# Attention gates of four heads in one product with tokens in the rows, and all heads' probabilities turned by VectorE, in a fused decoder layer on one Trainium2 core

## The chip, the core and the metric

The kernel runs on one core of one Trainium2 chip. The core has a matrix engine (TensorE, PE in the profile; its weight loads are PEld), and VectorE (DVE), ScalarE (ACT), GpSimd (POOL) and SyncE (SP), which here only issues transfers. The program lists the instructions of each engine in an order of its own; the engines meet at semaphores. Operands lie in on-chip memory with 128 partitions; products land in PSUM, in banks of 128 x 512 float32. POOL's and SP's transfers run on 16 DMA engines.

The metric is the time of one execution on the device in microseconds. Before the change the runs gave a median of 1040.27 us (1040.1 to 1040.35, three runs).

## What is computed

One decoder layer for 256 tokens of width 2048, in float32. What matters here is the attention and its gate; the convolution branch, the merge and the output projection stay as they are.

```python
h = rmsnorm(x, pre_norm_g)
proj = h @ w_in     # q_a 512, c_kv 512, k_rope 64, z_mla 2048, four of 2048 for the convolution, g_mla, g_conv
q = rmsnorm(q_a, q_a_norm_g) @ w_q_b        # 16 heads of 128 + 64
kv = rmsnorm(c_kv, kv_a_norm_g) @ w_kv_b    # 16 heads of 128 (keys) + 128 (values)
p = softmax(causal((q_nope @ k_nope.T + rope(q_rope) @ rope(k_rope).T) / sqrt(192)))
attn = (p @ v) * silu(z_mla)                # per head 256 x 128
y_mla = attn @ w_o_mla
y_conv = (b_gate * conv3(c_gate * c_in) * silu(z_conv)) @ w_o_conv
merged = sigmoid(g_mla) * y_mla + sigmoid(g_conv) * y_conv
return x + rmsnorm(merged @ w_out, post_norm_g)
```

## The kernel before

**Numbers in two halves.** A float32 operand goes into TensorE as a high part, rounded by a copy on ScalarE (`whi`, `hi`), and a low part, the difference, made by VectorE (`wlo`, `lo`). `split_act` (L232) issues the two; VectorE's needs ScalarE's. A `product` (L217) is three matmuls: high by high, high by low, low by high. `halves` (L224) does the same with both halves of the moving operand side by side in 512 columns: one matmul 512 wide and one 256 wide. The first kind of result is complete in a bank; the second lies in two halves of a bank, which `whole` (L378) adds up: a copy of one half by ScalarE (`half`) and an addition by VectorE.

**Weights.** Everything that is multiplied from `w_in`, `w_q_b` and the rest comes in units of 128 x 2048 (1 MB). `plan` (L106) lists them in the order of use. `take(i)` (L203) calls `ahead` (L192): SP has loaded units up to three on (`raw`, three buffers), and units up to one on are split, as two halves of 128 x 1024, into `whi` and `wlo`, five buffers of each (L186, L187). A split of a half can start when its buffer's last reader, a matmul, is done.

**Which order holds.** All of TensorE's instructions are kept in the order of the program (L88), POOL's transfers of the loop too, and the operations that are marked with `keep_in_program_order`. The rest of ScalarE's and VectorE's instructions is put in order by the scheduler of the framework, from its own estimate of times; the order is fixed when the program is built. Buffers are chosen from pools with a fixed number of them, and an operation waits until the one it gets is free.

**The loop.** After the latent projections (`qa`, `ckv`, `kr`) comes the loop over 16 heads (L739). The convolution's four projections have 2048 columns each, and 16 blocks of 512 columns of these are spread over the loop: `channels(h, i)` (L666), i = 0 to 3, is a quarter of the block that belongs to head h, 24 matmuls for each i and two banks `cv` (one for each 128 tokens). After the fourth quarter `channels_done` (L681) takes the banks away: block n = 0 of four by a ScalarE copy, n = 1 and 3 by a VectorE product, n = 2 by a ScalarE sigmoid and a VectorE product. For head h the program has

1. `project` (L387): the product for z of this head, features in the rows and both halves of the tokens in the columns, 16 matmuls 512 wide and 16 of 256, and `silu` (L654): `whole`, `rows` (the norm's factor), a sigmoid on ScalarE, a product.
2. `scores(h)` (L582) and the softmax behind it, on ScalarE and VectorE. From head 2 on the probabilities p are turned (tokens from rows to columns) by `turned` (L304): VectorE transposes blocks of 32 x 32 into `via`, `go` sends it to DRAM by four transfers of POOL (`far`), and `come` brings it back by one into p; `by_rows` and `quarters` are views that put the blocks in place. For heads 0 and 1 three transposes on TensorE do it (`tp`, L631).
3. `channels(h, 0)`, then `values(h - 1)` (L640) of the head before: four matmuls over pt and vv, then `whole` into `at_f` and a product with the gate `sz`.
4. `channels(h, 1)`, `come` for p, `channels(h, 2)`.
5. `made[h]`: the operands of coming heads (`group_a` queries and keys of two heads, `group_r` their rotary part, `group_v` the values of four heads).
6. `channels(h, 3)`, and `turn(h, p)` (L627), which splits the turned p into the halves `pt` (ScalarE, then VectorE; both kept in the program's order).

For the last head of each four (h % 4 == 3) `turn` comes ahead of step 5, and `values(h)` follows in step 5 right behind `group_a`; for head 15 values come at the end of the loop. In between stand the convolution's steps, `taps` (L702) and `channels_join` (L693), which turns a finished block by the same `turned`.

After the loop come the merge (`sq`, L857) and the output projection (`out`, L898). `split_branch` (L814) splits `at_f` there, two heads in one pass.

Of the kernel before, what the change touches and what calls it, by code (L numbers as in the profile page):

```python
# [18 lines left out]
P = 128  # L19
S = 256  # L20
# [62 lines left out]
def tile_layer(ctx: ExitStack, tc: tile.TileContext, xw, x, pos, pvec, post_g, wc, wz, wcv, wkr, wqk, wqr, wv, cwr, wsq, out):  # L83
# [6 lines left out]
    def transpose(*a):  # L90
        return tc.keep_in_program_order(nc.tensor.transpose(*a))  # L91
# [16 lines left out]
    def add(ap, width=UNIT):  # L108
        plan.append((ap, width))
        return len(plan) - 1  # L110
# [5 lines left out]
    u_head, u_grp = [[0] * 5 for _ in range(H)], {}  # L116


    made = {h: [] for h in range(H)}
# [6 lines left out]
    first = [("a", 0), ("r", 0), ("v", 0)]  # L126
    order = []
    for h in range(H):
        order += [(h, 0), (h, 1)] + (first if h == 0 else []) + [(h, 2), (h, 3)] + made[h] + [(h, 4)]
    for i, j in order:  # L130
        if i in ("a", "r", "v"):
            u_grp[i, j] = add({"a": wqk, "r": wqr, "v": wv}[i][j], R if i == "r" else UNIT)
        else:

            u_head[i][j] = add(wcv[i, j - 1] if j else wz[i])

    u_d = [[[add(wsq[n, c, k]) for k in range(4)] for n in range(4)] for c in range(4)]

# [64 lines left out]
    def take(i):  # L203
        ahead(i)
        parts = splits.pop(i)

        def piece(j, n):
            o = j * n
            h, o = o // HALF, o % HALF
            return parts[h][0][:, o : o + n], parts[h][1][:, o : o + n]  # L210

        return piece

    def bank(name, tag="mm", bufs=4):
        return psum.tile([P, 512], F32, name=name, tag=tag, bufs=bufs)
# [88 lines left out]
    def turned(src, via, n):  # L304

        via = via[:, : P * n]
        v = via.rearrange("p (q k x) -> p q k x", q=4, k=n)
        nc.vector.transpose(v.rearrange("p q k x -> p k q x"), src)  # L308
        far = dram.tile([P, P * n], F32, name="far", tag=f"far{n}", bufs=2)

        def go():
            f = far[:, :].rearrange("(q y) (i m) -> i y q m", q=4, i=4)
            for i in range(4):
                m = via[32 * i : 32 * i + 32, :].rearrange("y (q m) -> y q m", q=4)
                tc.keep_in_program_order(nc.gpsimd.dma_start(out=f[i], in_=m))  # L315

        def come(dst):

            tc.keep_in_program_order(nc.gpsimd.dma_start(out=dst, in_=far[:, :]))

        return go, come
# [260 lines left out]
    def scores(h):  # L582
# [35 lines left out]
        for t in range(NT):  # L618
            o = slice(t * P, (2 * t + 1) * P)
            nc.vector.tensor_scalar(p[:, o], p[:, o], rs[:, t : t + 1], None, op0=ALU.mult)  # L620
        if h < 2:
            return p, None
        go, come = turned(p[:, :], temp("via", (P, 3 * P), bufs=1), 3)
        go()
        return p, come

    def turn(h, p):  # L627

        pt = temp("pt", (P, 2, 3 * P), F32R, 1)
        if h < 2:  # L630
# [9 lines left out]
    def values(h, pt, sz):  # L640
# [12 lines left out]

    def silu(name, ps):  # L654
        f, s = temp("sl_f", bufs=1), temp(name)
        whole(f[:, :], ps)
        rows(f[:, :])
        nc.scalar.activation(s[:, :], f[:, :], AF.Sigmoid)
        nc.vector.tensor_tensor(s[:, :], f[:, :], s[:, :], op=ALU.mult)
        return s  # L660


    cv_t = cv_f[:, :, :].rearrange("p (j t k) s -> p j t (k s)", j=4, t=NT)
    cv_ps = {}

    def channels(h, i, between=None):  # L666

        if i == 0:
            cv_ps["now"] = [bank(f"cv{h}_{t}", tag="cv", bufs=2) for t in range(NT)]
        w = take(u_head[h][1 + i])  # L670
        for t in range(NT):
            if t and between:
                between()
            for k4 in range(4):
                k = 4 * i + k4
                a = [x_both[:, k, o + t * P : o + (t + 1) * P] for o in (0, S)]
                product(cv_ps["now"][t][:, :], a, w(k4, 512), k == 0, k == KD - 1)
        if i == 3:
            channels_done(*divmod(h, 4))

# [55 lines left out]

    cv_w = bp.tile([P, NT, 512], F32, name="cv_w")
    tap, coming = None, []
    for h in range(H):  # L739

        tapped = h % 4 == 2 or (h > 0 and h % 4 == 0) or h == H - 1
        sz_new = silu("sz", project(u_head[h][0], f"z{h}"))
        if h == 0:
            latent_turn("qa", qa, "q_g", (("st", 1), ("o", 1)))

            def turn_keys():
                latent_turn("ckv", ckv, "kv_g", (("mm", 4), ("mm", 4)))
                next(table_parts)

            channels(h, 0, turn_keys)  # L750
            for i in first:
                make(*i)
            key_rope()
            channels(h, 1)
            channels(h, 2)
            p, _ = scores(h)
        elif h == 1:

            pt = turn(0, p)
            channels(h, 0)  # L760
            values(0, pt, sz)
            p, _ = scores(h)
            channels(h, 1)
            channels(h, 2)
            pt = turn(h, p)
        else:
            p, come = scores(h)
            while coming:
                coming.pop()()
            channels(h, 0)  # L770
            if h > 2 and h % 4:

                values(h - 1, pt, sz)
            channels(h, 1)
            if tapped:
                next(tap)
            come(p[:, :])
            channels(h, 2)
            if tapped:
                next(tap)  # L780
            if h % 4 == 3:
                pt = turn(h, p)
        for i in made[h]:
            make(*i)
            if i[0] == "a" and (h == 1 or h % 4 == 3):
                values(h, pt, sz_new)
        sz = sz_new
        channels(h, 3)
        if h > 1 and h % 4 != 3:
            pt = turn(h, p)  # L790
        if h == H - 1:
            values(h, pt, sz)
        if h % 4 == 0 and h > 0:
            coming.append(channels_join(h // 4 - 1, 0))
        if h % 4 == 3:
            coming.append(channels_join(h // 4, 1))
        if h % 4 == 1:
            tap = taps(h // 4, 1)
            next(tap)
        elif h % 4 == 3 and h + 1 < H or h == H - 2:  # L800
            tap = taps(h // 4, 0)
            next(tap)
    coming.append(channels_join(3, 0))
    for come in coming:
        come()


    bstack.close()
# [5 lines left out]
    def split_branch(i):  # L814

        for h in (4 * i, 4 * i + 2):
            hs = slice(h, h + 2)
            split_act(at_both[:, hs, :S], at_both[:, hs, S:], at_f[:, hs, :], True)

    def split_turned(src, both, c, t):  # L820
        ks, ts = slice(4 * c, 4 * c + 4), slice(t * P, (t + 1) * P)
        lo = slice(t * P + S, (t + 1) * P + S)
        split_act(quarters(both[:, ks, ts]), quarters(both[:, ks, lo]), by_rows(src, 4), True)

    def split_channels(i):

# [221 lines left out]
```

## Time and profile before

| | before |
|---|---|
| median of the runs | 1040.27 us (1040.1 to 1040.35) |
| the profiled execution | 1040.44 us, span 1038.7 us |
| mean granted clock of TensorE | 0.998 |
| VectorE, ScalarE instructions | 984, 773 |

The time of an execution is its span, from the first to the last instruction in the trace, and some 1.7 us around it. In the profile a line such as `L234 DVE TENSOR_TENSOR pt<-p,pt 128x384 ...` names the line of the kernel, the engine, the operation, the tile it writes and those it reads; the numbers are microseconds, except the mean of one instruction, which is in ns. As helpers record nearly every operation, all matmuls have line 88 and all splits lines 233 and 234, and instructions are told apart by the names of their tiles. In a timeline the bracket at the end is the idle time of the engine ahead of the instruction and what ended it. Matmuls are pipelined: from the start of one to the start of the next can be less than the duration printed.

### The profile page before, as it was taken

What the parts mean: (1) busy time and instruction counts of PE and PEld (TensorE: products, weight loads), DVE (VectorE), ACT (ScalarE), POOL (GpSimd) and SP (SyncE); (2) the same over time, 40 slices, a digit from 0 to 9 for tenths busy, and PEclk for the clock granted to TensorE, in tenths of its full rate; (3) what the DMA queues carried; (4) which work ended last, traced back from release to release, by engine and by line L of the source; (5) the groups of instructions that cost most, each with busy time, mean ns of one, the idle gap of its engine ahead of it and who ended that gap; (6) DMA issues with size and microseconds to landing.
All of it is one profiled execution on the core that took longest, in us unless ns stands there. A gap on an engine that the chain in (4) does not pass through costs nothing.

```text
span 1038.7 us, 13002 instructions
## 1 busy us (share of the span) xinstructions
PE 1029.7 (99%) x4828; PEld 864.6 (83%) x4828; DVE 687.1 (66%) x984; ACT 561.0 (54%) x773; POOL 153.4 (15%) x295
## 2 busy tenths in 40 slices
PE   9999999999999999999999999999999999999996
PEld 8888888888888888888888888888888888888885
DVE  7588768777787787867877865564465455445562
ACT  7776656556565566565656565444334434443451
POOL 7620020032201321113122120020020001002000
PEclk9999999999999999999999999999999999999999
DMA  8755565586666766656768566565566556558642
GB/s 336 293 184 203 200 193 203 196 288 207 208 223 212 242 218 216 243 204 194 266 227 273 198 206 230 181 232 201 202 201 210 198 203 232 183 192 332 232 165 81
DMA packets 39903, 226.06 MB, mean 218 GB/s; under 512 B 6720, under 2 KB 7424, under 8 KB 16928
## 3 DMA queue, kind: packets, MB, share of 16 engines
q1 hardware_dynamic: 29808, 197.54, 53.6%
q0 software_dynamic: 9600, 24.40, 7.9%
q10 hardware_dynamic: 432, 3.29, 0.8%
q8 instruction: 38, 0.62, 0.2%
q14 instruction: 25, 0.20, 0.1%
HBM read 211.99 MB, written 9.04 MB: 213 GB/s over the span
## 4 chain that ended last, share of the span: by engine, by line
PE 99%; DVE 0%; ACT 0%; DVEq 0%; POOL 0%; issue 0%; POOLq 0%
PE cv L88 34%; PE sq L88 34%; PE z L88 9%; PE out L88 8%; PE qa L88 2%; PE kn L88 2%; PE qn L88 2%; PE vv L88 2%; PE ckv L88 2%; PE sc L88 1%; PE qr L88 1%; PE o L88 1%; PE idle L88 0%; PE kr L88 0%; DVE og L935 0%; PE lt_ckv L91 0%
## 5 line engine op out<-in xcount | busy, mean ns | idle before, releaser
L234 DVE TENSOR_TENSOR wlo<-raw,whi 128x1024 fp32r<-128x1024 f32 (+1 forms) x370 | 439.9, 1197 | 266.4 <-ACT whi L233 246.1
L233 ACT ACTIVATE whi<-raw 128x1024 fp32r<-128x1024 f32 (+1 forms) x372 | 381.8, 1035 | 361.6 <-PE sq L88 179.8
L88 PE MATMUL cv<-whi,x_both 128*128 128x512 f32 x1024 | 323.3, 390 | 0.0
L88 PEld LDWEIGHTS cv<-whi,x_both 128*128 128x128 f32 x1024 | 192.4, 188 | 39.0
L88 PE MATMUL cv<-wlo,x_both 128*128 128x512 f32 x512 | 199.7, 390 | 0.0
L88 PE MATMUL sq<-whi,x_both 128*128 128x512 f32 x512 | 158.4, 389 | 0.0
L88 PEld LDWEIGHTS sq<-whi,x_both 128*128 128x128 f32 x512 | 96.1, 188 | 19.9
L88 PEld LDWEIGHTS cv<-wlo,x_both 128*128 128x128 f32 x512 | 96.2, 188 | 18.7
L88 PE MATMUL sq<-wlo,x_both 128*128 128x512 f32 x256 | 99.7, 390 | 0.0
L88 PE MATMUL sq<-whi,at_both 128*128 128x512 f32 x256 | 79.5, 389 | 0.0
L88 PE MATMUL sq<-whi,cv_both 128*128 128x512 f32 x256 | 79.5, 389 | 0.0
L88 PE MATMUL out<-whi,m_both 128*128 128x512 f32 x256 | 79.1, 389 | 0.0
L315 POOL DMA_DIRECT2D far<-sg x32 | 17.5, 552 | 315.4 <-DVE sg L308 241.8
L88 PE MATMUL z<-x_both,whi 128*128 128x512 f32 x256 | 60.7, 390 | 0.0
L88 PEld LDWEIGHTS sq<-whi,at_both 128*128 128x128 f32 x256 | 48.1, 188 | 10.0
L88 PEld LDWEIGHTS sq<-whi,cv_both 128*128 128x128 f32 x256 | 48.1, 188 | 10.0
L88 PEld LDWEIGHTS out<-whi,m_both 128*128 128x128 f32 x256 | 48.1, 188 | 9.9
L88 PEld LDWEIGHTS sq<-wlo,x_both 128*128 128x128 f32 x256 | 48.1, 188 | 9.9
L88 PEld LDWEIGHTS z<-x_both,whi 128*128 128x128 f32 x256 | 48.0, 188 | 9.9
L315 POOL DMA_DIRECT2D far<-via x56 | 30.8, 556 | 142.4 <-DVE via L308 142.4
L88 PE MATMUL sq<-wlo,at_both 128*128 128x512 f32 x128 | 49.9, 389 | 0.0
L88 PE MATMUL out<-wlo,m_both 128*128 128x512 f32 x128 | 49.8, 389 | 0.0
(218 smaller groups left out, 1142.9 us busy)
## 6 DMA issues: line engine op xcount, KB each, us to landing
raw<-wsq_dram SPq DMA_DIRECT2D x80, 1024.0 KB, 4.7
raw<-wcv_dram SPq DMA_DIRECT2D x64, 1024.0 KB, 5.3
raw<-wz_dram SPq DMA_DIRECT2D x16, 1024.0 KB, 4.8
raw<-wqk_dram SPq DMA_DIRECT2D x8, 1024.0 KB, 4.8
cw<-cwr_dram POOLq DMA_DIRECT2D x24, 256.0 KB, 7.1
raw<-wc_dram SPq DMA_DIRECT2D x4, 1024.0 KB, 10.0
raw<-wv_dram SPq DMA_DIRECT2D x4, 1024.0 KB, 4.7
far<-via POOLq DMA_DIRECT2D x56, 48.0 KB, 4.0
```

The lines of the kernel that those rows point to most:

```text
L88: return tc.keep_in_program_order(nc.tensor.matmul(*a, **kw))
L233: a = nc.scalar.activation(hi, src, AF.Copy)
L234: b = nc.vector.tensor_tensor(lo, src, hi.bitcast(F32), op=ALU.subtract)
L315: tc.keep_in_program_order(nc.gpsimd.dma_start(out=f[i], in_=m))
```

## The change

The gate z is no longer made head by head. `gates(v, i)`, i = 0 to 3, is a quarter of the product for the four heads of group v, with the tokens in the rows and 4 x 128 features in the columns, by the same loop as the channels (now `quarter`); its two banks come from the pool `mm`. `gates_done(v)` makes silu of it, for each 128 tokens a ScalarE sigmoid of 128 x 512 and one VectorE pass, turns the result in the way of the probabilities (`turned`, and `come` later), and so leaves it in `at_f`, block by block where the heads' outputs will be. `values` adds up its bank into a temporary f and multiplies it in place into the gate. `split_branch` reads `at_f` through the turned view, with as many passes as before.

The gates of a group stand ahead of the first head of the four, with the steps of `taps` and `channels_join` that used to stand in that head. The order within a head is now scores, first quarter, values of the head before, and so on; for head 0 the first makings stand ahead of the first quarter. All heads' probabilities go through `turned`; the transposes on TensorE for heads 0 and 1 are gone. The DRAM buffers of `turned` are four of each size and not two. The order of the weight units in `plan` follows, and `wz` is laid out by blocks of 512 columns on the host.

```diff
     for h in range(H):
-        order += [(h, 0), (h, 1)] + (first if h == 0 else []) + [(h, 2), (h, 3)] + made[h] + [(h, 4)]
+        if h % HV == 0:
+            order += [("z", 4 * (h // HV) + i) for i in range(4)]
+        order += (first if h == 0 else []) + [(h, 0), (h, 1), (h, 2)] + made[h] + [(h, 3)]
...
-        far = dram.tile([P, P * n], F32, name="far", tag=f"far{n}", bufs=2)
+        far = dram.tile([P, P * n], F32, name="far", tag=f"far{n}", bufs=4)
...
-    def project(u, name, both=x_both, **kw):
-        w = take(u)
-        ps = bank(name, **kw)
-        halves([(ps, w(k, P), both[:, k, :], k == 0, k == KD - 1) for k in range(KD)])
-        return ps
...
-    def turn(h, p):
+    def turn(p):

         pt = temp("pt", (P, 2, 3 * P), F32R, 1)
-        if h < 2:
-            tp = bank(f"tp{h}", tag="st", bufs=1)
-            for b in range(3):
-                transpose(tp[:, b * P : (b + 1) * P], p[:, b * P : (b + 1) * P], ident[:, :])
-            split_act(pt[:, 0, :], pt[:, 1, :], tp[:, : 3 * P])
-            return pt
...
-        whole(at_f[:, h, :], o)
-        nc.vector.tensor_tensor(at_f[:, h, :], at_f[:, h, :], sz[:, :], op=ALU.mult)
...
+        at = at_t[:, h // HV, :, :].rearrange("p t (i k x) -> p t i k x", i=4, k=HV)[:, :, :, j, :]
+        f = temp("f")
+        whole(f[:, :], o)
+        nc.vector.tensor_tensor(at, f[:, :].rearrange("p (t i x) -> p t i x", t=NT, i=4), at, op=ALU.mult)
...
+    def gates(v, i, between=None):
+        if i == 0:
+            z_ps["now"] = [bank(f"z{v}_{t}") for t in range(NT)]
+        quarter(z_ps["now"], take(u_gate[v][i]), i, between)
+
+    def gates_done(v):
+        steps = []
+        for t in range(NT):
+            ps, g, r = z_ps["now"][t], at_t[:, v, t, :], r_col[:, t : t + 1]
+            nc.scalar.activation(g, ps[:, :], AF.Sigmoid, scale=r)
+            nc.vector.scalar_tensor_tensor(g, ps[:, :], r, g, op0=ALU.mult, op1=ALU.mult)
+            go, come = turned(g, temp("cw", (P, 512), bufs=2), 4)
+            go()
+            steps.append((come, g))
+        return [lambda come=come, g=g: come(g) for come, g in steps]
...
     for h in range(H):
-        sz_new = silu("sz", project(u_head[h][0], f"z{h}"))
...
+        v, last_of_four = divmod(h, HV)[0], h % HV == HV - 1
+
+        tapped = h % HV == 2 or h == H - 1
+        if h % HV == 0:
+            for i in range(4):
+                if v:
+                    gates(v, i)
+                    if i == 0:
+                        arrive()
+                    elif i < 3:
+                        next(tap)
...
+            if v:
+                coming.append(channels_join(v - 1, 0))
+            coming += gates_done(v)
         if h == 0:
...
             for i in first:
                 make(*i)
...
+        p, come = scores(h)
+        arrive()
+        if h:
             channels(h, 0)
-            if h > 2 and h % 4:
-
-                values(h - 1, pt, sz)
-            channels(h, 1)
...
+        if h % HV:
+
+            values(h - 1, pt)
+        channels(h, 1)
+        if tapped:
+            next(tap)
+        come(p[:, :])
+        channels(h, 2)
+        if tapped:
+            next(tap)
+        if last_of_four:
+            pt = turn(p)
         for i in made[h]:
             make(*i)
+            if i[0] == "a" and last_of_four:
+                values(h, pt)
         channels(h, 3)
-        if h > 1 and h % 4 != 3:
-            pt = turn(h, p)
-        if h == H - 1:
-            values(h, pt, sz)
+        if not last_of_four:
+            pt = turn(p)
+        elif h == H - 1:
+            values(h, pt)
```

More of the change, by code (lines that the diff above doesn't have):

```diff
@@ L115, in tile_layer @@
     u_kr = add(wkr, HALF)
-    u_head, u_grp = [[0] * 5 for _ in range(H)], {}
+    u_gate, u_head, u_grp = [[0] * 4 for _ in range(NV)], [[0] * 4 for _ in range(H)], {}
     made = {h: [] for h in range(H)}
@@ L650, in values, with quarter @@
         mm(both[:, :, P:], vv[0][:, 1, vs], pt[:, :, S:], start=False, stop=True)
-        whole(at_f[:, h, :], o)
-        nc.vector.tensor_tensor(at_f[:, h, :], at_f[:, h, :], sz[:, :], op=ALU.mult)
[L654 to L670, printed above, removed]
+        at = at_t[:, h // HV, :, :].rearrange("p t (i k x) -> p t i k x", i=4, k=HV)[:, :, :, j, :]
+        f = temp("f")
+        whole(f[:, :], o)
+        nc.vector.tensor_tensor(at, f[:, :].rearrange("p (t i x) -> p t i x", t=NT, i=4), at, op=ALU.mult)
+    at_t = at_f[:, :, :].rearrange("p (v t k) s -> p v t (k s)", v=NV, t=NT)
+    z_ps = {}
+    def quarter(pss, w, i, between=None):
         for t in range(NT):
@@ L676, in channels @@
                 a = [x_both[:, k, o + t * P : o + (t + 1) * P] for o in (0, S)]
-                product(cv_ps["now"][t][:, :], a, w(k4, 512), k == 0, k == KD - 1)
+                product(pss[t][:, :], a, w(k4, 512), k == 0, k == KD - 1)
+    def gates(v, i, between=None):
[12 more added lines that the diff above has]
+        return [lambda come=come, g=g: come(g) for come, g in steps]
+    cv_t = cv_f[:, :, :].rearrange("p (j t k) s -> p j t (k s)", j=4, t=NT)
+    cv_ps = {}
+    def channels(h, i):
+        if i == 0:
+            cv_ps["now"] = [bank(f"cv{h}_{t}", tag="cv", bufs=2) for t in range(NT)]
+        quarter(cv_ps["now"], take(u_head[h][i]), i)
         if i == 3:
@@ L738, in tile_layer, with arrive, turn_keys @@
     tap, coming = None, []
+    def arrive():
+        while coming:
+            coming.pop(0)()
     for h in range(H):
-        tapped = h % 4 == 2 or (h > 0 and h % 4 == 0) or h == H - 1
-        sz_new = silu("sz", project(u_head[h][0], f"z{h}"))
-        if h == 0:
[L744 to L750, printed above, removed]
+        v, last_of_four = divmod(h, HV)[0], h % HV == HV - 1
[4 more added lines that the diff above has]
+                    gates(v, i)
+                    if i == 0:
+                        arrive()
+                    elif i < 3:
+                        next(tap)
+                elif i == 1:
+                    def turn_keys():
+                        latent_turn("ckv", ckv, "kv_g", (("mm", 4), ("mm", 4)))
+                        next(table_parts)
+                    gates(v, i, turn_keys)
+                else:
+                    gates(v, i)
+                    if i == 2:
+                        key_rope()
+                    if i == 0:
+                        latent_turn("qa", qa, "q_g", (("st", 1), ("o", 1)))
+            if v:
+                coming.append(channels_join(v - 1, 0))
+            coming += gates_done(v)
+        if h == 0:
@@ L799, in tile_layer @@
+        if h % HV == 1:
+            tap = taps(v, 1)
             next(tap)
-        elif h % 4 == 3 and h + 1 < H or h == H - 2:
-            tap = taps(h // 4, 0)
+        elif last_of_four and h + 1 < H or h == H - 2:
+            tap = taps(v, 0)
             next(tap)
     coming.append(channels_join(3, 0))
-    for come in coming:
-        come()
+    arrive()
     bstack.close()
@@ L823, in split_turned, with split_branch @@
         split_act(quarters(both[:, ks, ts]), quarters(both[:, ks, lo]), by_rows(src, 4), True)
+    def split_branch(i):
+        for t in range(NT):
+            split_turned(at_t[:, i, t, :], at_both, i, t)
     def split_channels(i):
```

50 lines of the change are left out of this document (8 added, 42 removed).

## The prediction

> **What bounds the kernel now.** I read the page first, then the waits of TensorE, then the chain of waits around one odd head, then the queues of ScalarE and VectorE around the places where the change puts a wait.
>
> ```profile
> span 1038.7 us, 13002 instructions
> PE 1029.7 (99%) x4828; PEld 864.6 (83%) x4828; DVE 687.1 (66%) x984; ACT 561.0 (54%) x773; POOL 153.4 (15%) x295
> PE 99%; DVE 0%; ACT 0%; DVEq 0%; POOL 0%; issue 0%; POOLq 0%
> ```
>
> TensorE is busy for 99% of the span and the chain that ended last is TensorE's in the same share. Its waits are one line:
>
> ```profile
> PE idle L88 <- POOL hpi L257: 1.1, 1, 1.1
> ```
>
> So in the 1029 us after the first matmul it waits for nobody. A kernel like this gains only by fewer or shorter matmuls, and any wait that a change puts in front of a matmul is added in full, since TensorE's order is the program's (every matmul is kept in it). What hides everything else is what TensorE has to do between an operand's making and its use. The chain of waits, for heads 6 and 7 (start, us, what):
>
> ```profile
> 297.88 5.54 PE z L88 x32
> 303.42 0.95 PE sc L88 x8
> 304.36 5.45 PE cv L88 x24
> 309.81 0.57 PE o L88 x4
> 310.38 10.92 PE cv L88 x48
> 321.30 2.77 PE qn L88 x16
> 324.07 2.79 PE kn L88 x16
> 326.86 0.58 PE o L88 x4
> ```
>
> A head is: its gate product z (5.54), its scores, a quarter of the channels (5.45), the values of the head before, two quarters, the makings of the next group, the last quarter.
>
> **What it removes from TensorE.** Sixteen z of 5.54 us go: 88.6 us. Four groups of 96 products 512 wide come; they are of the channels' kind, whose rate is
>
> ```profile
> 578.70 16.36 PE cv L88 x72
> ...
> 102.99 0.49 PE L91 MATMUL tp<-ident,p 128*128 128x128 f32 x3
> 103.23 0.48 PE L88 MATMUL cv<-whi,x_both 128*128 128x512 f32 x1
> ```
>
> so 96 × 16.36/72 = 21.8 us a group and 87.2 in all: 1.4 us less. The six transposes of heads 0 and 1 go: three hold TensorE from 102.99 to 103.23, so 0.5 us for both heads. Together −1.9 us, which alone is 1038.5 against the profiled execution's 1040.44 (its span of 1038.7 plus 1.7 outside it; the median of the runs is 1040.27, 0.2 lower). The other engines get less: sigmoids four to a group with one table load a group and not one nearly every head, and wide passes for narrow ones. At 66% and 54% that is worth nothing by itself.
>
> **What it adds in front of TensorE.** The z of a head stood between the last quarter of the head before and its own scores. While TensorE did it, ScalarE and VectorE had 5.5 us more to catch up with the splits of weights and the split of the probabilities (pt), which comes at the end of a head for three heads of four and is needed after the next head's first quarter. That distance falls from 5.54 + 0.95 + 5.45 = 11.9 us to 6.4. The scheduler has set the order of both engines anew; I read the order of their instructions in the changed program. In three kinds of place pt now stands *behind* an instruction that can only start when TensorE reaches the very place where it needs pt. Prices:
>
> ```profile
> L234 DVE TENSOR_TENSOR wlo<-raw,whi 128x1024 fp32r<-128x1024 f32 x352 | 427.7, 1223 | 265.9 <-ACT whi L233 245.7 <-PE z L88 9.2 <-PE qa L88 1.2
> L233 ACT ACTIVATE whi<-raw 128x1024 fp32r<-128x1024 f32 x352 | 369.6, 1058 | 359.8 <-PE sq L88 179.8 <-PE cv L88 118.6 <-PE out L88 20.7
> ...
> L234 DVE TENSOR_TENSOR pt<-p,pt 128x384 fp32r<-128x384 f32 x14 | 7.7, 551 | 0.0
> L233 ACT ACTIVATE pt<-p 128x384 fp32r<-128x384 f32 x14 | 7.2, 518 | 1.6 <-DMA p<-far 1.6
> ```
>
> (a) *The end of the loop, head 15.* The trace of before has this very queue with pt ahead of it:
>
> ```profile
> 594.89 0.39 PE L88 MATMUL o<-pt,vv_hi 128*128 128x512 f32 x1
> 595.09 1.06 ACT L233 ACTIVATE whi<-raw 128x1024 fp32r<-128x1024 f32 x1 [0.30 <-PE cv L88]
> 595.97 0.74 DVE L691 SCALAR_TENSOR_TENSOR cv_w<-cv,r_both,cv_w 128x512 f32<-128x512 f32 x1
> 596.63 1.21 DVE L234 TENSOR_TENSOR wlo<-raw,whi 128x1024 fp32r<-128x1024 f32 x1
> 597.76 0.42 DVE L382 TENSOR_TENSOR at_f<-o,half 128x256 f32<-128x256 f32 x1
> ```
>
> The whi that starts 0.20 after the values' first product waits for a buffer that the quarter just ended had been reading. In the changed program ScalarE's part of pt stands behind that whi, VectorE's behind its wlo. So pt starts on VectorE where at_f does, at 597.76, and ends 0.55 later: 598.31 − 594.89 = 3.4 us of waiting.
>
> (b) *Heads 4, 8, 12* (their values, after the first quarter of heads 5, 9, 13). ScalarE's pt is queued behind the first half of the weight unit that is used three units on, for which one of five buffers must come free, and it comes free with the last product of that same first quarter. From its end T: whi at T + 0.20, ended at T + 1.26, wlo holds VectorE to T + 2.4 (597.76 − 596.63 = 1.13 from one start to the next), pt to T + 2.95, and 0.1 to reach TensorE (half of the 0.20 above): 3.05 us, three times, 9.15. Not below 2.9.
>
> (c) *Heads 3, 7, 11* (values after the keys of the next group). Here before has pt well ahead and now it is behind the copy of the second half of kn:
>
> ```profile
> 322.31 0.51 ACT L233 ACTIVATE pt<-p 128x384 fp32r<-128x384 f32 x1
> ...
> 326.70 0.40 PE L88 MATMUL o<-pt,vv_hi 128*128 128x512 f32 x1
> ...
> 327.79 0.38 ACT L381 ACTIVATE half<-kn 128x256 f32<-128x256 f32 x1
> ...
> 328.18 0.75 DVE L234 TENSOR_TENSOR qn_lo<-f,qn_hi 128x256 fp32r<-128x256 f32 x2
> 328.85 0.75 DVE L382 TENSOR_TENSOR f<-kn,half 128x256 f32<-128x256 f32 x2
> ```
>
> kn ends as the values want to start, at 326.70. The copy is at 327.79, ScalarE's pt after it to some 328.6; VectorE has two qn_lo first and reaches pt at 328.85, ends it at 329.40: 2.7 us, three times, 8.1. If ScalarE has nothing else in the way, the copy starts 0.20 after kn and pt follows with 0.52 and 0.55: 1.6 each. I take the upper, since both engines have the same work there as before.
>
> (d) *Small ones.* Heads 3, 7 and 11 take the two banks of the channels over from a head whose results go through VectorE:
>
> ```profile
> 297.71 3.56 PE L88 MATMUL z<-x_both,whi 128*128 128x512 f32 x15
> ...
> 299.63 0.75 DVE L691 SCALAR_TENSOR_TENSOR cv_w<-cv,r_both,cv_w 128x512 f32<-128x512 f32 x1
> ```
>
> The second bank is free at 300.38; without z it is wanted after the scores and the first half of a quarter, at 297.71 + 0.95 + 2.7 = 301.4. That just holds; 0 to 1 each, I take 0.2, 0.6 in all. In the first group the makings come straight after the gates, and a bank for qr is freed behind the gates' evacuation (a sigmoid, a product, a turn and weight splits): from 0 to 2.5 (two wlo), I take 0.8 as most of it can go on under the 5.5 us of the keys' and queries' products (2.77 + 2.79).
>
> The rest is covered: the gates' turn and its transfers are wanted a whole head later; two passes of VectorE on heads 0 to 15's outputs are replaced by one with a copy; weight units are as many as before, in another order.
>
> **Sum**: 1040.44 − 1.9 + 3.4 + 9.15 + 8.1 + 0.6 + 0.8 = 1060.6; less the 0.2 by which the profiled execution lies over the median: 1060.4, 20 us slower. By the lower ends (2.9, 8.7, 4.8, 0, 0): 1054.7; by the upper ones of (c) and (d): 1064.
>
> **Rivals.**
> *1. No wait, only the gain: 1038.3.* The mechanism is the 0.95 + 5.45 us that are left between a head's end and its values: pt needs p in place and 1.1 us of two engines, so it would fit with 5 to spare. It decides where pt is ahead of the buffer-bound whi in both queues: the values then start on time and the 1.9 us stay. For it: pt waits 1.6 us in the whole of before. Against it: the order I read, in which an engine doesn't step over a waiting instruction. The half-way case, some of the places on time, lies at 1041 to 1052.
>
> *2. p itself is late.* In before POOL issues a head's four scattering transfers and the gathering one:
>
> ```profile
> 311.65 2.19 POOL L315 DMA_DIRECT2D far<-via  x4 [23.76 <-DVE via L308]
> 318.54 0.57 POOL L319 DMA_DIRECT2D p<-far  x1 [4.69 <-DMA far<-via]
> ```
>
> 6.9 us from the first issue to the gather's, and more until it lands. With the gates' eight and the join's four ahead of the first head's four, 16 issues at 0.55 are 8.8 us for POOL alone. Head 4's p has its scores, three quarters and the next head's first (28 us) to arrive, so it should; if it is late by 1 to 3 us at (b), three times: 1063.5 to 1069.5.
>
> *3. The waits cost clock.* Granted clock is the number ahead of the DMA share:
>
> ```profile
> 6.77:1030.90 1024.13, 1024.10 (x4807) 859.26 (x4805) 680.97 (x973) 556.67 (x765) 149.14 (x277) 1.00 0.63 218
> 1030.90:1034.10 3.20, 0.00 (x0) 0.00 (x0) 2.44 (x6) 0.98 (x3) 0.00 (x0) 1.00 0.10 36
> 1034.20:1038.70 4.50, 0.00 (x0) 0.00 (x0) 1.09 (x2) 0.00 (x0) 0.00 (x0) 0.50 0.54 204
> ...
> 4.99 1.99 PE L88 MATMUL qa<-whi,x_both 128*128 128x512 f32 x4
> ...
> 7.28 1.08 PE L88 MATMUL qa<-whi,x_both 128*128 128x512 f32 x4
> ```
>
> The clock holds for 3.2 us after the last matmul and is half from 3.3 on. A wait of 3.3 us or more would thus be followed by matmuls at half pace, as at the start, where four products held TensorE for 1.99 and a little later for 1.08. There TensorE begins at 1.1 (its only wait) and runs at full pace by 7.3, so a fall costs at most half of 6.2, 3.1 us. At (a) the wait is 3.4 us, at (b) 3.05, just short: 0 to 12 us on top, up to 1072. The Trainium skill ("TensorE: Matmul & The Clock Gate", Part 1) has the same mechanism, with an idle window of about 3.4 us and as long a busy one until the clock is back; by its figures a fall would cost an estimated 1.7 us, so 1062 with head 15's alone and 1067 with all four. The trace agrees with the fall; of a return after a wait inside the kernel before shows nothing.
>
> **Chances.** My sum, 1054 to 1065: 66%. Late p or a lost clock, 1062 to 1072: 18%. Some of the places on time, 1041 to 1052: 9%. No wait at all: 7%, of which about half falls below the line, since −1.9 us is almost exactly 0.2%, about what a measurement of this kernel can tell from no change. So faster 4%, same 4%, slower 92%. The range is 1050 to 1070: it leaves out the top of the third group, most of the half-way cases and the gain alone.
>
> **What would show it.** In the profile of the changed kernel TensorE should wait for VectorE's pt at o: seven long waits, 3 us at heads 4, 8, 12, 2.7 at 3, 7, 11, 3.4 at 15, and its busy time should be some 2 us lower. z in a group should be 21.8 us. ScalarE's pt should start right behind a whi that waited for cv (b), and behind half<-kn (c). A clock under 1.00 after these waits speaks for rival 3; a pt that waits for the DMA of p, for rival 2. If TensorE has no wait at o, (a) to (c) are wrong and rival 1 holds; if it waits at sc or qn for a bank instead, (d) is too small.

## The result and the profile after

The changed kernel takes 1076.36 us (median of six runs, 1073.73 to 1080.41), the kernel before 1040.31 beside it: a ratio of 1.0347, 95% interval 1.0327 to 1.0368. It is slower, as forecast, but by 36 us where 20 were forecast, and over the range of 1050 to 1070. The profiled execution took 1080.41 us, the highest of the six. Its page, first the span, then the engines, then the chain that ended last:

```profile
span 1078.6 us, 12716 instructions
PE 1044.6 (97%) x4694; PEld 867.4 (80%) x4694; DVE 683.9 (63%) x954; ACT 535.1 (50%) x733; POOL 180.1 (17%) x345
PE 90%; DVE 4%; DMA 3%; ACT 1%; issue 1%; POOL 0%; DVEq 0%; ACTq 0%; POOLq 0%
```

TensorE is no longer the whole chain, and although it has fewer products (4694 for 4828) it is busy for 14.9 us more than before. Its waits, but for the 1.1 us at the start (us in total, times, longest):

```profile
PE o L88 <- DVE pt L238: 24.4, 7, 5.2
PE qr L88 <- DVE f L386: 0.3, 1, 0.3
```

Seven waits at o for VectorE's pt, at heads 3, 4, 7, 8, 11, 12 and 15. The chain of waits around the values of head 3 (start, us, what) is the forecast queue, nearly step for step:

```profile
189.17 2.80 PE kn L88 x16
...
192.41 0.27 ACT half L385
...
192.99 0.28 ACT half L385
...
193.28 0.75 DVE qn_lo L238 x2
194.03 0.48 DVE pt L238
...
194.65 1.41 PE o L88 x4
```

kn ends at 191.97, o starts at 194.65: 2.7 us. At head 8 the same view shows something else on the chain:

```profile
401.84 8.02 DMA p<-far
...
409.88 0.53 ACT pt L237
...
410.44 0.57 DVE pt L238
...
411.05 1.43 PE o L88 x4
```

Here pt waits for p itself, whose gathering transfer is issued at 401.84 and lands 8 us later; o starts 5.2 us late. And the granted clock falls. Four stretches around head 3's wait (length, busy us of PE, PEld, DVE, ACT, POOL, then the clock, 1.00 for full and 0.50 for half, the DMA share and GB/s):

```profile
190.62:194.03 3.41, 1.34 (x10) 1.09 (x8) 2.51 (x6) 2.62 (x6) 0.00 (x0) 1.00 1.00 394
194.03:197.45 3.42, 2.80 (x8) 2.44 (x9) 2.75 (x8) 1.13 (x3) 0.00 (x0) 0.50 0.18 74
197.45:200.86 3.41, 3.41 (x9) 2.64 (x9) 0.01 (x1) 0.00 (x0) 0.00 (x0) 0.50 0.00 0
200.86:204.28 3.42, 3.42 (x16) 2.80 (x16) 1.36 (x2) 2.06 (x3) 0.00 (x0) 1.00 0.00 0
```

In the third stretch TensorE does nine matmuls in the time in which it does sixteen at full clock. Each of the seven waits is followed by one such stretch or, at heads 3, 8 and 12, two: ten in all.

The account of this execution: 1038.5 for the gain alone, 24.4 of waits, and 16.8 by which TensorE's busy time (1044.6) lies over 1029.7 − 1.9: 1079.7, against 1080.4. Of the 16.8, some 15 belong to the ten stretches at half clock, in which TensorE is busy for 30.2 us and would be for half as long at full clock; the rest I haven't placed. The gain itself is there: a group's gates take

```profile
209.28 21.76 PE z L88 x96
```

### The profile page after: what moved, and what is told of

It is laid out like the page before. It is cut to its first block, busy times and chain, and to the rows that moved or that the text cites. A ratio compares the mean times of both kernels' runs of the same rounds, so it can differ in the third digit from the quotient of the medians.

```text
span 1078.6 us, 12716 instructions
## 1 busy us (share of the span) xinstructions
PE 1044.6 (97%) x4694; PEld 867.4 (80%) x4694; DVE 683.9 (63%) x954; ACT 535.1 (50%) x733; POOL 180.1 (17%) x345
## 4 chain that ended last, share of the span: by engine, by line
PE 90%; DVE 4%; DMA 3%; ACT 1%; issue 1%; POOL 0%; DVEq 0%; ACTq 0%; POOLq 0%
PE sq L88 32%; PE cv L88 28%; PE out L88 8%; PE z L88 8%; PE vv L88 2%; PE qa L88 2%; PE ckv L88 2%; PE kn L88 2%; PE qn L88 2%; DMA p<-far 1%; PE o L88 1%; PE sc L88 1%; DVE wlo L238 1%; DMA far<-mv 1%; ACT whi L237 1%
## 5 line engine op out<-in xcount | busy, mean ns | idle before, releaser
L88 PE MATMUL cv<-whi,x_both 128*128 128x512 f32 x1024 | 327.2, 394 | 0.4
L88 PEld LDWEIGHTS cv<-whi,x_both 128*128 128x128 f32 x1024 | 195.0, 190 | 41.2 <-DVE cv_w L699 1.0
L88 PE MATMUL z<-whi,x_both 128*128 128x512 f32 x256 | 80.1, 390 | 0.0
L319 POOL DMA_DIRECT2D far<-via x64 | 35.2, 557 | 160.0 <-DVE via L312 159.9
L88 PEld LDWEIGHTS z<-whi,x_both 128*128 128x128 f32 x256 | 48.1, 188 | 9.9
L88 PE MATMUL z<-wlo,x_both 128*128 128x512 f32 x128 | 49.8, 389 | 0.0
```

The lines of the kernel that those rows point to most:

```text
L88: return tc.keep_in_program_order(nc.tensor.matmul(*a, **kw))
```

## The experiments

All are edits of the changed kernel unless said otherwise. Times are medians, with the ratio to the kernel before on the same chip. A profile is of one execution: for e1, e2, e7 and e10 the longest of their runs, for e3, e9 and e12 the shortest. Where an edit leaves an engine's queue alone, the scheduler has still set the order of ScalarE and VectorE anew.

| run | median us | ratio (95%) | waits of TensorE in its profile, us (times), but for the 1.1 at the start |
|---|---|---|---|
| e1_pt_first | 1069.78 | 1.0278 (1.0261 to 1.0296) | o 22.1 (7), sc 0.5, qr 0.3 |
| e2_pool | 1064.61 | 1.0230 (1.0207 to 1.0253) | o 18.4 (7), cv 0.8, qr 0.3 |
| e3_both | 1055.84 | 1.0153 (1.0135 to 1.0170) | o 9.6 (4), qr 0.3 |
| e5_later | 1046.15 | 1.0052 (1.0034 to 1.0070) | cv 4.0 (3), qr 0.3, qa 0.2 |
| e6_later_r | 1040.23 | 1.0007 (0.9998 to 1.0017) | sc 0.6, qr 0.3 |
| e7_z_ahead (of before) | 1065.75 | 1.0248 (1.0232 to 1.0264) | o 14.7 (4), tp 2.8, qa 0.3 |
| e8_both_r | 1049.64 | 1.0087 (1.0072 to 1.0102) | o 5.1 (2), cv 3.4 (3), qr 0.3 |
| e9_v_first | 1044.03 | 1.0050 (1.0030 to 1.0069) | sc 2.7, qa 0.8 |
| e10_v_first_pool | 1043.04 | 1.0029 (1.0018 to 1.0040) | sc 2.7, o 0.8, qa 0.2 |
| e11_later_r_pool | 1039.72 | 1.0000 (0.9991 to 1.0009) | o 1.2, qr 0.3 |
| e12_r_first_pool | 1041.36 | 1.0014 (1.0005 to 1.0023) | vv 1.0, kn 0.8 |
| e4_clock (of before) | 1168.99, one run | | hold 85.8 (14) |

### Is it the order of the queues, or p? (e1, e2, e3)

e1 makes the instructions that stood ahead of pt follow it on ScalarE and VectorE: the weight halves of heads 4, 8, 12 and 15 and of the next gates, the copy of the next group's qn, and the last product of the convolution at head 15.

```diff
+    def behind_pt(a, b):
+        for i, p in zip((a, b), pt_now):
+            if i is not None:
+                tc.add_manual_dep(i.ins, p.ins.name, ...)
...
-            split_act(hi[:, :n], lo[:, :n], t[:, h : h + n])
+            ab = split_act(hi[:, :n], lo[:, :n], t[:, h : h + n])
+            if (i, h) in after_pt:
+                behind_pt(*ab)
```

> The changed kernel with the splits pt put ahead, in the queues of ScalarE and VectorE, of the instructions that wait for TensorE (a weight half, the copy of qn, the convolution's last product); TensorE's and POOL's order unchanged. Theory A (queue order makes all seven waits, and each costs clock besides): no waits at o are left, 1038.5 to 1040 us. Theory B (queue order at heads 3, 7, 11, 15; at heads 4, 8, 12 it is p that lands late, at 1.8, 4.4 and 2.9 us after the values were due in the profile of the changed kernel): the four waits of the first kind go with their clock, the three of the second kind stay at 2.9 to 5.4 us with 6.7 us of clock in all, about 1038.3 + 12.8 + 6.7 = 1058 us. Theory C (waits are a symptom, the new gates or their transfers slow something else): stays near 1076.

Neither A nor B came: in the profiled execution all seven waits stayed, 22.1 us of 24.4, and at each of the seven ScalarE, with those instructions now behind pt, stands idle for 3.4 to 7.7 us until p's transfer lands. The median fell by 6.6 us. The profiled execution, 1077.94 us, is 7.7 us longer than the next of the five, so the others may have waited less.

e2 edits none of those queues and moves the gates' eight scattering transfers on POOL behind the four of p, and their gathering ones behind p's.

```diff
             go, come = turned(g, temp("cw", (P, 512), bufs=2), 4)
-            go()
-            steps.append((come, g))
+            steps.append((go, come, g))
...
         p, come = scores(h)
-        arrive()
+        if h % HV:
+            arrive()
+        else:
+            for go, _, _ in steps:
+                go()
...
         come(p[:, :])
+        if h % HV == 0:
+            arrive()
+            for _, c, g in steps:
+                c(g)
```

> The changed kernel with POOL's order alone changed: the gates' eight scattering transfers are issued behind those of the first head's p, and the gates' and the convolution's gathering ones behind p's. p of heads 4, 8, 12 then lands some 7 us earlier. Theory B: their waits fall to the 3.05 us that the queue order alone makes, the other four stay: waits 9.2 + 8.6 + 4.2 = 22 us against 25.5, clock some 1 to 3 us less: 1070 to 1074. Theory A: the same, since the queue order hides p's lateness at head 4 and explains 3.05 at each. If p's lateness were the only cause at heads 4, 8, 12: 1056 to 1060.

It does more than A and B expected: 11.8 us. The waits at heads 4, 8 and 12 fall to 1.6 us each, under the 3.05 that I had worked out for the queues, and the clock doesn't fall after them; the one at head 7 grows from 2.7 to 4.1, as p lands later there. But 1.6 is not what the queues alone cost in the changed kernel. There two weight halves stand ahead of head 4's pt on ScalarE, and in e2, at the same place, the scheduler has put pt between them:

```profile
261.66 1.06 ACT L237 ACTIVATE whi<-raw 128x1024 fp32r<-128x1024 f32 x1 [0.29 <-PE cv L88]
263.24 0.52 ACT L237 ACTIVATE pt<-p 128x384 fp32r<-128x384 f32 x1 [0.52 <-DMA p<-far]
```
```profile
258.75 0.51 ACT L237 ACTIVATE pt<-p 128x384 fp32r<-128x384 f32 x1
259.16 1.04 ACT L237 ACTIVATE whi<-raw 128x1024 fp32r<-128x1024 f32 x1
```

So e2 takes away p's lateness and half of the queue together. In the changed kernel VectorE is done with the second half 2.4 us after the values were due, at heads 4, 8 and 12 alike; with pt behind it that is a wait of 2.9, near the 3.05 forecast, and the measured ones are 2.9, 5.2 and 4.2. By this estimate p's lateness adds nothing at head 4, 2.3 us at head 8 and 1.3 at head 12. In the changed kernel POOL's queue shows why p is late (head 8's group; start, us, what):

```profile
383.98 2.22 POOL L319 DMA_DIRECT2D far<-mv  x4 [11.68 <-DVE mx L607]
386.19 2.18 POOL L319 DMA_DIRECT2D far<-cw  x4
...
394.13 0.55 POOL L319 DMA_DIRECT2D far<-cw  x1 [1.54 <-DMA far<-mv]
394.75 2.18 POOL L319 DMA_DIRECT2D far<-via  x4
...
401.84 0.54 POOL L323 DMA_DIRECT2D p<-far  x1 [0.91 <-DMA far<-via]
```

The first eight transfers, four of the join and four of the gates, go out one behind another. The gates' other four are issued one by one, each when one of the join's has landed (the bracket), and only then p's: 10.8 us from 383.98 to 394.75, where twelve issues of 0.55 are 6.6. I had counted 8.8 us for POOL's sixteen issues and nothing for these waits.

e3 has both edits.

> Both edits together. Theories A and B: no waits at o, granted clock 0.997 or more, 1038.3 to 1040 us, which is the gain of 1.9 us that the shorter products promised. Theory C: over 1050.

1055.84 us is what C expected (over 1050), not A or B. The waits at heads 4, 8 and 12 are gone; those at 3, 7, 11 and 15 stay, 2.0 to 3.5 us, though nothing stands ahead of pt any more. The profile of e3 at head 3:

```profile
187.24 0.56 POOL L334 DMA_DIRECT2D p<-far  x1 [5.22 <-ACT whi L248]
...
192.04 0.52 ACT L248 ACTIVATE pt<-p 128x384 fp32r<-128x384 f32 x1 [3.47 <-DMA p<-far]
```

ScalarE stands idle for 3.47 us and waits for p: it lands after the values are due there too, with the queues out of the way. So the order that the scheduler had chosen was not the only cause at these heads; freeing the queues uncovers the next thing that is late. e3 is also the first to show that equal waits can cost differently: those at heads 3, 7 and 11 are alike, and the clock falls after the second alone (below).

### Why p is late (e8, e5, e6)

In before, head 7's p was issued at 318.54, and the view of the tile p there has, from issue to landing,

```profile
DMA to landing us min/median/max: 3.5/3.5/3.5
```

so it landed 17.7 us after the scores' end (304.36), and the values were due 22.3 us after it (326.70). The chain starts late now. In the changed kernel, head 7, TensorE's last score and VectorE's queue:

```profile
314.19 0.40 PE L88 MATMUL sc<-kr,qr 128*128 128x256 f32 x2
```
```profile
316.06 0.74 DVE L699 SCALAR_TENSOR_TENSOR cv_w<-cv,r_both,cv_w 128x512 f32<-128x512 f32 x1
316.73 0.55 DVE L238 TENSOR_TENSOR pt<-p,pt 128x384 fp32r<-128x384 f32 x1
317.19 1.22 DVE L238 TENSOR_TENSOR wlo<-raw,whi 128x1024 fp32r<-128x1024 f32 x1
318.44 0.87 DVE L238 TENSOR_TENSOR qr<-f,qr 64x256 fp32r<-64x256 f32 x2
319.34 0.29 DVE L600 TENSOR_TENSOR p<-sc,sc_half 128x128 f32<-128x128 f32 x1
```

and the same two places in before:

```profile
303.96 0.40 PE L88 MATMUL sc<-kr,qr 128*128 128x256 f32 x2
```
```profile
305.52 0.28 DVE L602 TENSOR_TENSOR p<-sc,sc_half 128x128 f32<-128x128 f32 x1
```

VectorE reaches the softmax 5.15 us after the last scores began, where it was 1.56: what the head before left to it (the rotation of qr, the taking away of cv, the last pt, weights) it used to do under z. e8 tests that: e3 with the rotary part of heads 2, 6, 10 and 14 made one quarter earlier.

```diff
         come(p[:, :])
+        if h % HV == 2:
+            for i in made[h]:
+                make(*i)
...
         channels(h, 2)
```

> The changed kernel with pt first in the queues and POOL's order changed, as in the run with both edits, and the rotary part of heads 2, 6, 10, 14 made one quarter earlier; the values stay in their place. Theory D (at heads 3, 7, 11 p lands late because VectorE reaches the softmax 4 us later, behind the rotary part): the waits of 2.2 us there go, the one at head 15 (3.7 us, with 2.8 of clock) stays: 1045 to 1048 us. Theory E (the transfers themselves have become slower): 1053 to 1057 as in that run.

The waits of heads 7 and 11 go, those of 3 and 15 stay (2.0 and 3.1 us; 5.1 in the waits' view), and three waits at cv come, of 3.4 us in all: 1049.64, 6.2 us less than e3 and a little over what D allowed. D holds at two heads of three; why heads 3 and 15 keep theirs I haven't settled.

e5 edits neither the queues nor POOL's order and gives the cover back in TensorE's own order: values one quarter later, or behind vv.

```diff
+        channels(h, 1)
         if h % HV:
 
             values(h - 1, pt)
-        channels(h, 1)
...
-            if i[0] == "a" and last_of_four:
+            if i[0] == "v":
                 values(h, pt)
```

> The changed kernel with the values moved in TensorE's order: those of the head before stand behind the second quarter of the channels and not the first, and those of heads 3, 7 and 11 behind the next group's values and not its keys: 5.45 us of cover again, as z gave. Queue orders are left to the scheduler. Theories A and B: the waits at heads 3, 4, 7, 8, 11, 12 go, since the work behind which pt stands is done within 3.1 us and p lands within 5.4 us; at most one wait, at head 15, is left: 1038.5 to 1040 without it, 1044 with it. Theory C: over 1050.

No wait at o is left, at head 15 neither. 30 of the 36 us are gone with TensorE's work rearranged and nothing taken away, though 1046.15 is over the 1038.5 to 1040 expected. What is left is my small item (d), and one fall of the clock behind the longest of its waits:

```profile
PE cv L88 <- DVE cv_w L699: 4.0, 3, 2.0
```

The banks of the channels at heads 3, 7 and 11, behind the same rotation on VectorE; I had put them at 0.2 us each. e6 adds the earlier rotary part of e8.

> The changed kernel with the values moved as in the run before, and the rotary part of the next group at heads 2, 6, 10, 14 made one quarter of the channels earlier, so that its VectorE passes are done before the head ends. Theory D (z's 5.5 us were what VectorE worked off its backlog in): no waits at o, the waits at cv of heads 3, 7, 11 (1.5, 2.2 and 0.8 us in the run before) fall to 0.3 or less, the wait at qr of 0.5 stays, no fall of the clock: 1039.0 to 1040.3 us. Theory that the channels' banks wait for something else (the convolution's transfers): 1042 to 1046 as before.

1040.23 us: the three waits at cv are gone and the kernel is level with before (1.0007, 0.9998 to 1.0017).

### Place or form? (e7)

The kernel before, with its own z per head, but the four of a group ahead of the group. The temporary of silu shares a buffer with the rotation's to make room.

```diff
-        order += [(h, 0), (h, 1)] + ...
+        order += ([(h + k, 0) for k in range(HV)] if h % HV == 0 else []) + [(h, 1)] + ...
...
-        sz_new = silu("sz", project(u_head[h][0], f"z{h}"))
+        if h % HV == 0:
+            szs = [silu("sz", project(u_head[h + k][0], f"z{h + k}")) for k in range(HV)]
+        sz_new = szs[h % HV]
```

> The kernel before with the gates still made head by head in its own form (features in the rows, nothing turned, no transfers for them), but the four z of a group moved ahead of the group's first head, where the changed kernel has them; probabilities as before. Theory D (place): waits at o of heads 3, 7, 11 of about 2.8 us and at cv of 1 to 2 us, and some at 4, 8, 12 or 15, with clock lost behind them: 1052 to 1068 us. Rival F (form: what costs is the turned product of four heads, its transfers and its multiplication in place): 1040 to 1043 us.

1065.75 us, 25 us over before, with no gate turned and no transfer added (what the shared buffer costs by itself I haven't tested). Its waits:

```profile
PE o L88 <- DVE pt L234: 14.7, 4, 6.6
PE tp L91 <- ACT cv_f L686: 2.8, 1, 2.8
```

Three of the four at o are those of heads 3, 7 and 11 with the changed kernel's own length, 2.7 us, the fourth is head 15's; heads 4, 8 and 12 have none. So the place of z is enough for all but these three. Theirs need something of the form, either the gates' transfers on POOL or the place of pt: in e7 pt stands ahead of the weight halves that wait for the quarter before the values (at head 4 it starts on ScalarE at 259.35, the first of these halves at 263.87), so e7 doesn't tell the two apart.

### What a wait costs in clock (e4)

The kernel before with a wait put behind the last quarter of heads 1 to 14.

```diff
+    def wait_a_while(h, n):
+        o = bank(f"hold{h}", tag="o", bufs=1)
+        matmul(o[:, :LINE], ones[:, :], ones[:, :LINE], start=True, stop=True)
+        tc.keep_in_program_order(nc.vector.tensor_copy(hold[:, :], o[:, :LINE]))
+        for _ in range(n):
+            tc.keep_in_program_order(nc.vector.tensor_scalar(hold[:, :], hold[:, :], 0.5, None, op0=ALU.mult))
+        matmul(o[:, LINE : 2 * LINE], ones[:, :], hold[:, :], start=True, stop=True)
```

> The kernel before, with a wait of TensorE put behind the last quarter of heads 1 to 14: a small matmul, a chain of 3 to 16 short VectorE operations over its result, and a small matmul that needs the chain's end; waits of some 1 to 3.3 us, rising from head to head. The outputs are those of before. Theory G (read from the changed kernel and the four runs above): the granted clock is set anew every 3.41 us, and falls to half after a stretch of that length in which TensorE idled for more than about half, so some waits under 3.3 us cost one or two stretches at half pace: no fall up to waits of 1.7 us, a fall nearly always from 2.7 us, by their place against the stretches in between. Theory H (what I took in the prediction, a wait has to last 3.3 us): no fall at any of them, mean clock 0.998 as before.

The waits came out longer than meant, from 3.3 to 8.2 us, as other work got between, so that the falls of all 14 don't rule out H by themselves. But all changes of the clock lie on a grid of 3.41 us, in each of the profiles, and the stretches in which a wait begins or ends show how much idleness it takes. Two neighbouring stretches of e4 and then two of e2 (same columns as above):

```profile
471.38:474.79 3.41, 1.61 (x9) 1.26 (x7) 2.38 (x5) 2.12 (x2) 0.51 (x1) 1.00 0.01 1
474.79:478.20 3.41, 0.00 (x0) 0.00 (x0) 3.06 (x13) 0.00 (x0) 2.70 (x5) 1.00 0.80 217
478.20:481.62 3.42, 3.41 (x9) 2.83 (x10) 0.42 (x1) 0.00 (x0) 0.00 (x0) 0.50 0.48 170
```
```profile
473.33:476.75 3.42, 1.43 (x11) 1.14 (x9) 2.52 (x7) 2.62 (x6) 0.00 (x0) 1.00 1.02 405
476.75:480.16 3.41, 2.71 (x8) 2.36 (x9) 2.74 (x8) 1.14 (x3) 0.00 (x0) 0.50 0.23 94
```

With 1.61 us of work in a stretch (1.80 idle, 53%) the clock is still full in the next one; with 1.43 (1.99 idle, 58%) it is half. Once the clock is up, in none of these profiles does it stay full behind a stretch with more idle time than 1.88 (55%, at the end of e12), or fall behind one with less than 1.94 (57%, in e10). It comes back after a stretch that is busy nearly throughout: 0.42 us of idle time in a stretch at half clock (e4) kept it half, 0.30 (e7) did not. So a wait of 2 us that falls into one stretch costs clock, and one that lies across two may not. In e3 the waits at heads 3 and 7 are both some 2 us:

```profile
191.95:195.37 3.42, 2.07 (x11) 1.79 (x12) 2.51 (x5) 3.17 (x8) 0.00 (x0) 1.00 0.58 242
328.49:331.90 3.41, 1.41 (x8) 1.26 (x9) 1.85 (x4) 2.67 (x7) 0.00 (x0) 1.00 0.81 318
```

Head 3's has 0.74 us in the stretch before the first line and 1.34 in it, and costs nothing; head 7's has its 2.0 in the second line alone, and the next stretch at half clock costs 1.7 us. A wait of 2.7 us that e9 and e10 have at the same place does the same: in e9 it is 1.37 and 1.31 us of two stretches and the clock stays, in e10 1.94 of one and the clock is half for two. G holds in this, though no wait of e4 is short enough to try its lower end; H falls. The Trainium skill ("TensorE: Matmul & The Clock Gate", Part 1) gives a window of about 3.4 us, and the 3.41 agree; that a whole window must be idle is not what these runs show, 57% of one is enough.

### A version that beats both? (e9 to e12)

e6 has a wait of 0.3 us at qr in the first group, and single runs up to 1043.7. e9 puts the first group's values ahead of its queries (`first = [("v", 0), ("a", 0), ("r", 0)]`), e10 is e9 with e2's order on POOL, e11 is e6 with it, e12 is e11 with the first rotary part ahead (`first = [("r", 0), ("a", 0), ("v", 0)]`).

> The kernel of the run with later values and earlier rotary part, with the first group's values made ahead of its queries and keys, so that the bank that qr takes is freed before VectorE is at the gates of the first group. Theory D: the wait of 0.5 us at qr goes, 0.5 us less than that run's 1040.2: 1039.3 to 1040.2 us, with single runs some 3 us higher where p lands late. If it doesn't go: 1040.2.

> The same with POOL's order changed too (the gates' transfers behind p's). If the high single runs of that kernel (1042 to 1043.7) come from p landing late at heads 4, 8 and 12, they go, and the median is 1038.8 to 1039.8 us, under before; if not, as the kernel beside it.

Neither reached the times hoped for: the wait at qr goes, and the scores of head 0 now wait 2.7 us for the rotation, which comes last. e10's profiled execution pays for it in clock too. Its runs go up to 1045.1, e9's to 1049.6.

> Values one quarter later, rotary part one quarter earlier, and POOL's order changed (gates' transfers behind p's); the first group's makings in their old order. If p landing late at heads 4, 8, 12 makes the high single runs (1042 to 1043.7) of the kernel without the change of POOL's order, they go, and the median is 1039 to 1040 us. If they come from head 15 (0.8 us of waiting there in the last profile), the spread stays and the median is 1040 to 1041.

> The same with the first group's rotary part made ahead of its queries and keys: qr takes a free bank, so the 0.5 us at qr go, and the rotation is done earlier, so the scores don't wait for it as they did with the values ahead (2.7 us): 0.5 us under the kernel beside it, 1038.5 to 1039.5 us. If a bank is missing elsewhere instead: as beside it or up to 2 us more.

e11 has a median of 1039.72 (1038.81 to 1042.74) and a ratio of 1.0000 (0.9991 to 1.0009): no gain that can be told. The median is the one expected if p at heads 4, 8 and 12 made the high runs, but high runs are still there; in its profile head 15 waits 1.2 us for pt. e12 moves the first group's wait to kn and vv and is at 1041.36. None of the twelve beats the kernel before.

## Why the prediction was right in sign and wrong in size

- **What bounds the kernel, and the gain.** Right: TensorE had no wait to give, 96 products take 21.76 us (21.8 forecast), and once the waits at o and their clock are nearly gone, in e6 and e11, TensorE is busy for 1028.3 us, 1.4 less than before. In the time nothing of this can be told from before, as one small wait or two remain (0.9 and 1.5 us).
- **The places of the waits.** Right: seven waits at o, at the seven heads named, 24.4 us where 20.65 were forecast. At heads 3, 7 and 11 each is 2.7 us as worked out; at 4, 8, 12 and 15 they are 2.9, 5.2, 4.2 and 4.0 for 3.05, 3.05, 3.05 and 3.4.
- **Their cause.** Right in part. (a) to (c) put them down to the order on ScalarE and VectorE. That order ends the waits of the changed kernel at heads 3, 4, 7 and 11, about as long as worked out, and at head 15, where VectorE has more ahead of pt than (a) has. At heads 8 and 12 rival 2 came on top: p lands later than the queues would have held pt. And behind the queues p is late at all seven heads: e1 takes the order away, and in its profile 22.1 of the 24.4 us are waited all the same. Head 4's p, I wrote, "has its scores, three quarters and the next head's first (28 us) to arrive, so it should"; it had 29.6 and didn't, since POOL's queue holds waits for landings and not issues alone. For heads 3, 7 and 11 I never asked whether p would be late, since their distance from scores to values did not change; the start of the softmax did, by 3.6 us (the profile, and e8 for two of the three).
- **The clock: the step that failed.** Rival 3 said a wait "of 3.3 us or more" costs clock and that 3.05 is "just short", and the sum took nothing for it. As a rival it had 0 to 12 us for four of the seven places. All seven waits cost clock, those of 2.7 us too: TensorE is busy for 16.8 us more in the profiled execution than the account above has for its work, some 15 of them in the half-clock stretches. The sum is 1060.6 for a profiled execution, 19.8 under the 1080.4 measured; this busy time is 16.8 of them, and waits longer than forecast (24.7 for 22.05) are 2.7. The border was read from the end of the kernel, where the clock fell 3.3 us after the last matmul; that shows how long an idle time can last before a fall, and not how short. By the grid it depends on where the last matmul lies: the same end comes 2.4 us after it in e6 and 5.3 in e12.
- **The small ones.** Forecast 1.4 us, measured 0.3. That they were small because o's waits gave VectorE time is a reading, not shown by itself; it fits e5, where these are gone and the banks of cv alone cost 4.0.

## What to carry to other kernels

Work of an engine that never waits is also cover for what follows it; before it is gathered into one place for a small gain, look for each chain of the other engines that ran under it, from its first instruction on and through every queue with landings in it. Undoing the queue order that a profile shows ahead of a late instruction proves little until the operand is shown to be there, and an edit of one queue can move another engine's, as in e2, so the queues are compared before a wait is put down to the edit. On this chip a wait of TensorE is priced with the clock: 2 us inside one 3.41 us stretch cost some 1.7 more (e3, head 7).

## What was not expected of the hardware

The granted clock changes on a fixed grid of 3.41 us in every profile here. A stretch with 1.94 us of idle time or more halves it for the next, one with 1.88 or less doesn't, and it returns only after a stretch that is nearly all busy (0.30 us of idle time let it return, 0.42 didn't). POOL's gathering transfers of p, 192 KB each, took from 2.6 to 8.0 us from issue to landing in the changed kernel, 3.9 in the median, and from 2.7 to 6.4 in before; why head 8's took 8.0 I haven't settled.
